# 128-row score matmuls, and the adaLN products spread over feed-forward and mixer blocks, in a two-layer macaron trunk

## The chip, the cores and the metric

The program runs on one core of one Trainium2 chip. The metric is device time in microseconds, the median of the runs shown; lower is better. Engines are named as in the profile: PE is TensorE (PEld its weight loads), DVE VectorE, ACT ScalarE, POOL GpSimd, SP SyncE, whose queue issues nearly all DMAs.

## What is computed

Two layers of three sub-layers each, on x of 512 tokens by 1024, in fp32:

```
c1 = silu(c)                                     # one vector of 1024
for l in range(2):
    mod = c1 @ ada_w[l] + ada_b[l]               # 9 vectors of 1024: (shift, scale, gate) per sub-layer
    for s in (0, 1, 2):
        h = x * (1 + scale[s]) + shift[s]
        if s == 1:  y = concat(NSA(h), gMLP(h), SSD(h)) @ w_out          # the mixer
        else:       y = (silu(h @ w1) * (h @ w3)) @ w2                    # hidden width 2816
        x = layer_norm(alpha*x + k * (1 + gate[s]) * y) * ln_g + ln_b     # k = 1 in the mixer, else 1/2
```

NSA is attention with 8 heads of 64 in 2 key groups and 3 branches: 31 compressed keys, selected blocks (here all that are causal), and a window. Each branch is softmax(q k + bias) v under a causal mask. All 18 adaLN vectors depend on c alone, so each may be made at any time before its use; together they read 75 MB of `ada_w`.

## The kernel before, in words

**Numbers.** Each fp32 matrix is split into a high and a low part, and a product is three matmuls (`mm3`, L121 to L123). Weights come as raw tiles of 128x1024 (512 KB); `wsplit` loads one (L88), optionally multiplies it by the gate row G on VectorE (L101), casts the high part on ScalarE (L103) and subtracts it on VectorE (L105). `wsplit_s` does it in two halves (L111, L116, L117). Raw tiles have four buffers in all, shared by weights and the `ada_w` tiles; the split parts have five each. Large rows (G, `lg`, `lb`, `csil`) take the eight buffers of pool `bp`.

**Sub-layers** run in the order n = 0 to 5: FFN, mixer, FFN, FFN, mixer, FFN.

**An FFN** (`ffn`) treats its 22 hidden tiles of 128 in two halves of 11. A half has an up phase, 11 tiles of 48 matmuls of 512 columns with the activation behind each (L292 to L298: tanh on ScalarE, L293, then `th`·h3 by L294, which frees the PSUM bank of h3, then the split into `ghi` and `glo`), and a down phase (`down`, L364 to L370), which multiplies by w2 with the gate row G folded in. The down phase of token block 1 accumulates into the two banks that held h3, so its first matmul waits for L294 of the last two tiles. The last four tiles of w2 are taken block by block, with `residual` or `post_norm` behind each block.

**The adaLN products.** One vector is eight products (`ada_vec`, L155): each loads 512 KB of `ada_w` and runs one VectorE instruction with c1 broadcast in `csil`, and a small instruction that reads its accumulator. A gate vector is then finished by L167, written to DRAM element by element (the DMA `mod<-mod`), and read back as a row broadcast over partitions (the DMA `G<-mod`, `gate_par`, scaled by L178). Two of the 18 vectors are made at the start, while the first tiles are fed (`feed`); the others by `bg`, a generator that the FFNs call once behind each up tile. `share` says how many vectors each sub-layer makes (seven in n=0, four in n=2, five in n=3), and `bg` makes `total` steps in 19 calls.

**A mixer** (`mixer`) projects, runs the SSD core, makes keys (`key`) and then scores, in 24 units of group p, query block and branch. A unit of the branches 1 and 2 scores four heads (L861, L862), each a pair of matmuls into one bank: K high, held in 128 rows against q high and q low, then K low in 64 rows against q high alone. There are 64 pairs in a mixer, 16 each of 512, 384, 256 and 128 columns. VectorE adds the bias and takes the maximum (L864), ScalarE exponentiates (L866), VectorE makes factors (L816 to L820) and scales (L874); TensorE transposes the result (L892) and multiplies by the values (L902). Scores are made two units ahead (LOOK). Between these, `tick` fits in other jobs: the rest of the input projections, the output projection, and a step that loads the norm rows and G (`params`).

Who stands where on each engine is settled by a scheduler that works by the program's order and its own estimates of durations; each engine then works strictly in that order, and so does each queue of DMAs.

## Time and profile before

| | before |
|---|---|
| median of 3 runs | 2165.61 us (2159.95 to 2165.88) |
| the profiled execution, its own time | 2163.19 us |
| its span, first to last instruction | 2161.5 us |
| TensorE busy | 2092.3 us, 97% |
| VectorE busy | 1344.4 us, 62% |
| ScalarE busy | 775.9 us, 36% |
| granted TensorE clock, mean | 0.989 |
| HBM read | 275.89 MB, 130 GB/s over the span |

Busy time is the sum of an engine's instructions in the span. Matmuls are pipelined, so the rate in matmuls per stretch says more of TensorE than its busy share.

### The profile page before, as it was taken

How to read it: one execution, taken by the hardware profiler on the slowest of the kernel's cores; microseconds unless marked ns; L12 is line 12 of the kernel's file. 1: busy time of each engine (PE TensorE's matmuls, PEld its weight loads, DVE VectorE, ACT ScalarE, POOL GpSimd, SP SyncE). 2: the span in 40 equal slices, each digit the busy share in tenths (PEclk: the TensorE clock that was granted, in tenths of full speed). 3: DMA queues.
4: the chain of work that ended last, by engine and by line, in shares of the span. 5: the costliest groups of instructions: out<-in, count | busy, mean ns of one | idle time of the engine just before them, and what ended most of it. 6: DMA issues, size and time to landing. Idle time of an engine off the chain costs nothing.

```text
span 2161.5 us, 26067 instructions
## 1 busy us (share of the span) xinstructions
PE 2092.3 (97%) x10024; PEld 1664.9 (77%) x10024; DVE 1344.4 (62%) x2416; ACT 775.9 (36%) x1351; POOL 29.0 (1%) x43
## 2 busy tenths in 40 slices
PE   7979997999999999999999899999999999999997
PEld 5868886887666788888888788888766668888886
DVE  6783666676767766356584736558777665444453
ACT  3321322534556622123252212225355564222222
POOL 0000000000000000000000000000000000000000
PEclk9989998999999999999999999999999999999999
DMA  9773874323211364364446527542241204223331
GB/s 334 222 236 94 230 251 130 101 88 136 79 59 40 108 218 133 97 179 153 146 138 169 171 89 225 127 127 88 88 141 59 64 1 137 90 97 98 97 97 40
DMA packets 93001, 279.74 MB, mean 129 GB/s; under 512 B 19235, under 2 KB 23587, under 8 KB 92876
## 3 DMA queue, kind: packets, MB, share of 16 engines
q1 hardware_dynamic: 92204, 275.43, 40.9%
q0 software_dynamic: 672, 2.64, 0.3%
q8 instruction: 79, 1.29, 0.2%
q14 instruction: 46, 0.38, 0.1%
HBM read 275.89 MB, written 4.76 MB: 130 GB/s over the span
## 4 chain that ended last, share of the span: by engine, by line
PE 77%; DMA 10%; DVE 8%; issue 3%; ACT 2%; POOL 0%; SPq 0%; DVEq 0%; POOLq 0%; ACTq 0%
PE h L122 10%; PE h L121 10%; PE h L123 10%; PE y L121 8%; PE y L123 8%; PE y L122 8%; DMA raw<-in_ada_w_dram 5%; DMA raw<-in_w_dram 4%; PE pj L121 3%; PE pj L122 3%; PE pj L123 3%; PE op L902 3%; PE tp L892 2%; DVE wlo L105 2%; PE S L862 2%
## 5 line engine op out<-in xcount | busy, mean ns | idle before, releaser
L103 ACT CAST whi<-raw 128x1024 fp32r<-128x1024 f32 (+1 forms) x306 | 318.1, 1046 | 682.5 <-PE h L122 196.3
L121 PE MATMUL h<-hT_hi,whi 128*128 128x512 f32 (+1 forms) x1488 | 559.1, 377 | 4.0 <-ACT hT_hi L1033 3.8
L122 PE MATMUL h<-hT_lo,whi 128*128 128x512 f32 (+1 forms) x1488 | 559.8, 376 | 0.3 <-DVE hT_lo L215 0.3
L123 PE MATMUL h<-hT_hi,wlo 128*128 128x512 f32 (+1 forms) x1488 | 559.3, 376 | 0.0
L105 DVE TENSOR_TENSOR wlo<-raw,whi 128x1024 fp32r<-128x1024 f32 (+1 forms) x306 | 370.5, 1215 | 203.4 <-ACT whi L103 203.0
L121 PEld LDWEIGHTS h<-hT_hi,whi 128*128 128x128 f32 x1488 | 280.0, 188 | 55.5 <-ACT hT_hi L1033 4.8
L122 PEld LDWEIGHTS h<-hT_lo,whi 128*128 128x128 f32 x1488 | 280.5, 188 | 51.9 <-DVE hT_lo L215 0.9
L123 PEld LDWEIGHTS h<-hT_hi,wlo 128*128 128x128 f32 x1488 | 280.4, 188 | 50.7
L155 DVE CUSTOM_DVE_ANT_0 raw<-raw,csil 128x1024 f32<-128x1024 f32 x144 | 174.8, 1221 | 156.4 <-DMA raw<-in_ada_w_dram 155.9
L121 PE MATMUL y<-whi,ghi 128*128 128x512 f32 x576 | 228.7, 397 | 32.1 <-DVE th L294 31.8
L122 PE MATMUL y<-wlo,ghi 128*128 128x512 f32 x576 | 227.1, 394 | 0.2 <-DVE wlo L105 0.2
L123 PE MATMUL y<-whi,glo 128*128 128x512 f32 x576 | 226.8, 394 | 0.0
L101 DVE TENSOR_TENSOR raw<-raw,G 128x1024 f32<-128x1024 f32 x86 | 104.7, 1222 | 88.3 <-DMA raw<-in_w_dram 88.3
L121 PEld LDWEIGHTS y<-whi,ghi 128*128 128x128 f32 x576 | 109.9, 191 | 59.2 <-DVE th L294 36.6
L297 ACT CAST ghi<-th 128x512 fp32r<-128x512 f32 x88 | 54.5, 620 | 213.2 <-DVE th L294 213.2
L122 PEld LDWEIGHTS y<-wlo,ghi 128*128 128x128 f32 x576 | 110.1, 191 | 23.4 <-DVE wlo L105 0.6
L123 PEld LDWEIGHTS y<-whi,glo 128*128 128x128 f32 x576 | 109.9, 191 | 23.3
L121 PE MATMUL pj<-hT_hi,whi 128*128 128x512 f32 x288 | 118.4, 411 | 0.0
L123 PE MATMUL pj<-hT_hi,wlo 128*128 128x512 f32 x288 | 113.4, 394 | 0.0
L122 PE MATMUL pj<-hT_lo,whi 128*128 128x512 f32 x288 | 113.2, 393 | 0.0
L294 DVE TENSOR_TENSOR th<-th,h 128x512 f32<-128x512 f32 x88 | 60.0, 682 | 41.7 <-PE h L123 40.9
L894 ACT COPY pt<-tp 128x512 f32<-128x512 f32 (+2 forms) x96 | 54.6, 581 | 85.4 <-PE tp L892 76.9
(290 smaller groups left out, 2569.3 us busy)
## 6 DMA issues: line engine op xcount, KB each, us to landing
raw<-in_w_dram SPq DMA_DIRECT2D x264, 512.0 KB, 3.6
raw<-in_ada_w_dram SPq DMA_DIRECT2D x144, 512.0 KB, 4.6
raw<-in_wS_dram SPq DMA_DIRECT2D x36, 512.0 KB, 3.8
raw<-in_cw_dram SPq DMA_DIRECT2D x16, 512.0 KB, 3.9
raw<-in_wo_dram SPq DMA_DIRECT2D x16, 512.0 KB, 3.6
T<-lane SPq DMA_DIRECT2D x16, 256.0 KB, 3.7
lg<-in_ln_g_dram SPq DMA_DIRECT2D x6, 512.0 KB, 6.0
lb<-in_ln_b_dram SPq DMA_DIRECT2D x6, 512.0 KB, 6.8
```

Source lines behind the costliest of these rows:

```text
L101: V.tensor_mul(raw, raw, gain)
L103: S.copy(hi[:, :n], raw[:, :n])
L105: V.tensor_sub(lo[:, :n], raw[:, :n], hi[:, :n].bitcast(F32))
L121: PE.matmul(o, lh, rh, start=first, stop=False)
L122: PE.matmul(o, lh, rl, start=False, stop=False)
L123: PE.matmul(o, ll, rh, start=False, stop=last)
L155: V.tensor_tensor_reduce(out=raw, in0=raw, in1=cond["c"], scale=0.5, scalar=0.0, op0=ALU.mult, op1=ALU.add, accum_out=acc[:, k:k + 1])
L294: V.tensor_mul(th, th, h3)
L297: S.copy(hi, th)
L862: PE.matmul(o, Q[g, i][r, qs], K[br][1][r, :nk], start=False, stop=True)
L894: S.copy(pt[0:n, :], tp[0:n, :])
L902: PE.matmul(op[r, :], v, pt[0:n, g * 256:(g + 1) * 256], start=(br == 0), stop=(br == 2 and kb == qb))
```

## The change

1. **Scores.** K low is made as a full tile of 128 rows in each group, the same 64 rows twice, so that both matmuls of a pair have 128 rows; the second one then adds q low times K low as well. This takes one more VectorE subtraction per half, eight in all in both mixers, and one buffer of `bp` for the second group's tiles.
2. **The adaLN products.** `share` becomes {0:4, 1:3, 2:3, 3:3, 4:3}: three vectors move into each mixer, and three FFNs make fewer. The steps of a sub-layer are dealt over 36 calls (n=0), 38 (other FFNs) or 18 (mixers); the calls come also in the down phases (seven a half, and behind each block's residual in the first), and behind each scoring unit. Each mixer makes its own `csil` ahead of its scores.
3. **Norm rows in the mixer.** `params` is split: the gate row is loaded at the place of before, the norm rows after `settle`, some steps later.

```diff
@@ ffn
                 for b in range(4):
                     down(f, w, b)
+                bg()
...
                 if half == 0:
                     residual(b, y[b], True)
+                    bg()
@@ mixer
-        Q, K = {}, {}
+        Q, K, k_lo = {}, {}, []
...
             kh = [slab("kh", dt=F32R), slab("kh", dt=F32R)]
-            kl = slab("kl", dt=F32R)
+            if not k_lo:
+                k_lo.extend(pair(bp.tile([128, 1024], F32R, tag="b", name=nm("kl"))))
+            kl = [slab("kl", dt=F32R), k_lo[br - 1]]
             for g, r, o in ((0, lo_half, hi_half), (1, hi_half, lo_half)):
                 S.copy(kh[g][r, :], ps[r, :])
-                V.tensor_sub(kl[r, :], ps[r, :], kh[g][r, :].bitcast(F32))
+                V.tensor_sub(kl[g][r, :], ps[r, :], kh[g][r, :].bitcast(F32))
+                V.tensor_sub(kl[g][o, :], ps[r, :], kh[g][r, :].bitcast(F32))
                 S.copy(kh[g][o, :], ps[r, :])
...
                 PE.matmul(o, Q[g, i][:, qs], K[br][0][g][:, :nk], start=True, stop=False)
-                PE.matmul(o, Q[g, i][r, qs], K[br][1][r, :nk], start=False, stop=True)
+                PE.matmul(o, Q[g, i][:, qs], K[br][1][g][:, :nk], start=False, stop=True)
...
             if n == GAIN_0:
-                jobs.append(step(params))
+                jobs.append(step(gate_params))
...
-        jobs += [step(settle), step(gains, range(9 - GAIN_0, 8))]
+        jobs += [step(settle), step(norm_params), step(gains, range(9 - GAIN_0, 8))]
...
+        silu_c()
         probs = [score(*u, TICK_0) for u in units[:LOOK]]
...
             else:
                 release()
+            bg()
@@ planning
-    share = {0: 7, 2: 4, 3: 5}
+    share = {0: 4, 1: 3, 2: 3, 3: 3, 4: 3}
...
+        slots = {0: 36, 1: 18, 4: 18}.get(n, 38)
...
-                if n == 0 and key == items[-3]:
+                if n == 0 and key == items[-2]:
                     yield from make_bias()
...
-            want = done[1] + 1 if more else min(total, done[0] * total // 19)
+            want = done[1] + 1 if more else min(total, done[0] * total // slots)
...
             need(l, s, 2)
-            if not last:
-                need(*subs[n + 1], 1)
-                need(*subs[n + 1], 0)
             cond.clear()
-            mixer(l, P, last, lane, params)
+            mixer(l, P, last, lane, make_bg(n, P), lambda: gate_par(l, s, P), lambda: norm_par(l, s, P))
```

How this moves instructions is shown at three places. In the rows, names end in running numbers, which differ between the kernels; a tile keeps its number from row to row of one kernel.

The first is SyncE's queue in the first half of n=0, round the first gate vector: `mod` is its write to DRAM, `G` its reading back; `raw<-in_ada_w_dram` loads for a product, `raw<-in_w_dram` a weight tile. Before, between the weights of the eighth up tile (`raw_799`, `raw_805`) and of the ninth (`raw_878`, `raw_884`) of the eleven:

```order
L88 DMA raw_746<-in_ada_w_dram 128x1024
L88 DMA raw_799<-in_w_dram 128x1024
L88 DMA raw_805<-in_w_dram 128x1024
L88 DMA mod_735<-mod_98_567 128x8x1
L88 DMA ab_741<-in_ada_b_dram 128x8
L88 DMA raw_819<-in_ada_w_dram 128x1024
L88 DMA G_737<-mod_735 128x1024
L88 DMA raw_822<-in_ada_w_dram 128x1024
L88 DMA raw_825<-in_ada_w_dram 128x1024
L88 DMA raw_878<-in_w_dram 128x1024
L88 DMA raw_884<-in_w_dram 128x1024
```

and now, where `raw_991` and `raw_997` are the weights of the eleventh and last up tile, and `raw_1086` and `raw_1126` tiles of w2:

```order
L88 DMA raw_938<-in_ada_w_dram 128x1024
L88 DMA raw_991<-in_w_dram 128x1024
L88 DMA raw_997<-in_w_dram 128x1024
L88 DMA raw_1011<-in_ada_w_dram 128x1024
L88 DMA raw_1086<-in_w_dram 128x1024
L88 DMA raw_1120<-in_ada_w_dram 128x1024
L88 DMA mod_1073<-mod_98_567 128x8x1
L88 DMA ab_1118<-in_ada_b_dram 128x8
L88 DMA G_1075<-mod_1073 128x1024
L88 DMA raw_1123<-in_ada_w_dram 128x1024
L88 DMA raw_1126<-in_w_dram 128x1024
```

The write and the reading back stood three up tiles ahead of the end of the up phase; they now stand behind its last weights, among the first tiles of w2.

The second is VectorE at the end of the up phase of the second half of n=0 (L294 is `th`·h3, L101 the product of w2 and G, L155 an adaLN product and its accumulator). Before, ahead of the last tile's L294 (`th_2387`):

```order
L101 TENSOR_TENSOR raw_2570<-raw_2570,G_737 128x1024
L298 TENSOR_TENSOR glo_2322<-th_2317,ghi_2321 128x512
L105 TENSOR_TENSOR wlo_2482<-raw_2477,whi_2480 128x1024
L105 TENSOR_TENSOR wlo_2513<-raw_2508,whi_2511 128x1024
L293 SCALAR_TENSOR_TENSOR th_2387<-th_2387,h_411_2337 128x512
L101 TENSOR_TENSOR raw_2601<-raw_2601,G_737 128x1024
L111 TENSOR_TENSOR raw_2632<-raw_2632,G_737 128x1024
L294 TENSOR_TENSOR th_2387<-th_2387,h_412_2338 128x512
L105 TENSOR_TENSOR wlo_2544<-raw_2539,whi_2542 128x1024
L298 TENSOR_TENSOR glo_2392<-th_2387,ghi_2391 128x512
```

and now, ahead of the last tile's L294 (`th_2282`):

```order
L155 ISA raw_2475,mod_374_2291<-raw_2475,csil_112 128x1024
L155 ISA mod_374_2291 128x1
L105 TENSOR_TENSOR wlo_2415<-raw_2410,whi_2413 128x1024
L293 SCALAR_TENSOR_TENSOR th_2282<-th_2282,h_368_2232 128x512
L101 TENSOR_TENSOR raw_2478<-raw_2478,G_1075 128x1024
L155 ISA raw_2509,mod_374_2291<-raw_2509,csil_112 128x1024
L155 ISA mod_374_2291 128x1
L167 SCALAR_TENSOR_TENSOR mod_374_2291<-mod_374_2291,ab_2292 128x8
L101 TENSOR_TENSOR raw_2515<-raw_2515,G_1075 128x1024
L294 TENSOR_TENSOR th_2282<-th_2282,h_369_2233 128x512
```

Before, only w2's products and splits stand round L293 and L294; now two adaLN products stand among them, and with the second L167, which ends a gate vector, two rows ahead of the last L294.

The third is VectorE in the first mixer's scores, in a unit with 128 columns. Before (L864 maximum, L816 to L820 factors, L874 scaling):

```order
L864 ISA P_4838,mx_4825<-S_4837,T_4003 128x128
L864 ISA mx_4825 128x1
L864 ISA P_4828,mx_4825<-S_4827,T_4000 128x128
L864 ISA mx_4825 128x1
L864 ISA P_4838,mx_4825<-S_4837,T_4006 128x128
L864 ISA mx_4825 128x1
L816 TENSOR_SCALAR sm_4826<-sm_4826 128x4
L817 RECIPROCAL sm_4826<-sm_4826 128x4
L820 TENSOR_TENSOR sm_4826<-sm_4826,gts_2964 128x4
L874 TENSOR_SCALAR P_4828<-P_4828,sm_4826 128x128
L874 TENSOR_SCALAR P_4838<-P_4838,sm_4826 128x128 x2
L225 SCALAR_TENSOR_TENSOR x_sb<-x_sb,y_4861 128x512
```

and now, where the same lines stand as L869, L822 to L826 and L879:

```order
L155 ISA raw_4900,mod_826_4712<-raw_4900,csil_3916 128x1024
L155 ISA mod_826_4712 128x1
L822 TENSOR_SCALAR sm_4783<-sm_4783 128x4
L155 ISA raw_4903,mod_826_4712<-raw_4903,csil_3916 128x1024
L155 ISA mod_826_4712 128x1
L823 RECIPROCAL sm_4783<-sm_4783 128x4
L155 ISA raw_4952,mod_826_4712<-raw_4952,csil_3916 128x1024
L155 ISA mod_826_4712 128x1
L826 TENSOR_TENSOR sm_4783<-sm_4783,gts_2878 128x4
L225 SCALAR_TENSOR_TENSOR x_sb<-x_sb,y_4818 128x512
L879 TENSOR_SCALAR P_4785<-P_4785,sm_4783 128x128
L879 TENSOR_SCALAR P_4795<-P_4795,sm_4783 128x128 x2
```

Three adaLN products stand between the maxima and the factors, so ahead of the scaling that TensorE's transposes take.

## Rows read from the trace of the kernel before

**Rows 1.** The page: the span, the busy time and count of each engine (section 1), and from section 2, the span in 40 slices of 54 us, the row of PE.
```profile
span 2161.5 us, 26067 instructions
...
PE 2092.3 (97%) x10024; PEld 1664.9 (77%) x10024; DVE 1344.4 (62%) x2416; ACT 775.9 (36%) x1351; POOL 29.0 (1%) x43
...
PE   7979997999999999999999899999999999999997
```

**Rows 2.** Busy time by stretch: from and to in us, its length, then for each engine busy us and in brackets how many instructions ran; the last three columns are the granted TensorE clock, the share of DMA and GB/s. First a steady stretch, then the start, then the three ends of an up phase at which TensorE ran fewer matmuls (behind each of the first two the next 40 us), and last such an end at which it did not.
```profile
200.00:240.00 40.00, 40.00 (x178) 33.14 (x177) 22.44 (x32) 8.67 (x10) 0.00 (x0) 1.00 0.62 164
0.00:40.00 40.00, 24.15 (x100) 18.95 (x101) 28.37 (x54) 16.09 (x21) 0.20 (x4) 1.00 1.00 357
120.00:160.00 40.00, 27.56 (x117) 21.88 (x116) 34.21 (x46) 11.22 (x14) 0.00 (x0) 0.87 0.66 224
160.00:200.00 40.00, 40.00 (x171) 32.90 (x171) 12.48 (x12) 7.36 (x7) 0.00 (x0) 0.96 0.30 93
320.00:360.00 40.00, 27.52 (x109) 21.73 (x108) 27.16 (x33) 8.49 (x11) 0.00 (x0) 0.80 0.53 153
360.00:400.00 40.00, 40.00 (x175) 33.04 (x174) 17.30 (x19) 10.45 (x14) 0.00 (x0) 0.98 0.41 126
1200.00:1240.00 40.00, 33.34 (x139) 27.09 (x138) 30.41 (x37) 10.92 (x14) 0.00 (x0) 0.91 0.49 158
840.00:880.00 40.00, 39.87 (x177) 32.67 (x176) 21.21 (x21) 9.43 (x11) 0.00 (x0) 1.00 0.32 95
```

**Rows 3.** TensorE's timeline at these three ends: start us, duration us, engine, line, operation and tiles; in square brackets how long the engine had stood idle before it, and what released it.
```profile
146.90 0.50 PE L121 MATMUL y<-whi,ghi 128*128 128x512 f32 x1 [1.44 <-DVE th L294]
158.69 0.80 PE L121 MATMUL y<-whi,ghi 128*128 128x512 f32 x1 [10.82 <-DVE th L294]
...
344.44 0.79 PE L121 MATMUL y<-whi,ghi 128*128 128x512 f32 x1 [3.04 <-DVE th L294]
355.52 0.80 PE L121 MATMUL y<-whi,ghi 128*128 128x512 f32 x1 [9.43 <-DVE th L294]
356.12 0.63 PE L122 MATMUL y<-wlo,ghi 128*128 128x512 f32 x1
356.54 0.63 PE L123 MATMUL y<-whi,glo 128*128 128x512 f32 x1
...
1230.93 0.79 PE L121 MATMUL y<-whi,ghi 128*128 128x512 f32 x1 [6.66 <-DVE th L294]
```

**Rows 4.** VectorE's timeline ahead of the second row of these (columns as in rows 3).
```profile
153.11 0.68 DVE L293 SCALAR_TENSOR_TENSOR th<-th,h 128x512 f32<-128x512 f32 x1
156.81 1.23 DVE L101 TENSOR_TENSOR raw<-raw,G 128x1024 f32<-128x1024 f32 x1 [1.89 <-DMA raw<-in_w_dram]
157.96 0.68 DVE L294 TENSOR_TENSOR th<-th,h 128x512 f32<-128x512 f32 x1
```

**Rows 5.** Groups of instructions by line and shape over the whole span: busy us in total, mean ns of one, then the engine's idle time just ahead of them and what ended most of it.
```profile
L155 DVE CUSTOM_DVE_ANT_0 raw<-raw,csil 128x1024 f32<-128x1024 f32 x144 | 174.8, 1221 | 156.4 <-DMA raw<-in_ada_w_dram 155.9
L583 DVE TENSOR_TENSOR kl<-pj,kh 64x512 fp32r<-64x512 f32 x8 | 5.5, 688 | 13.2 <-ACT kh L582 12.9
```

**Rows 6.** VectorE's timeline at the last products of one gate vector, and behind another one's (columns as in rows 3).
```profile
82.95 1.22 DVE L155 CUSTOM_DVE_ANT_0 raw<-raw,csil 128x1024 f32<-128x1024 f32 x1
84.09 1.22 DVE L155 CUSTOM_DVE_ANT_0 raw<-raw,csil 128x1024 f32<-128x1024 f32 x1
...
1183.85 1.23 DVE L155 CUSTOM_DVE_ANT_0 raw<-raw,csil 128x1024 f32<-128x1024 f32 x1 [12.15 <-DMA raw<-in_ada_w_dram]
```

**Rows 7.** The timeline of SyncE's DMA queue round a gate vector's write and its reading back: start us, us of issuing, engine, line, operation and tiles.
```profile
85.43 0.38 SPq L88 DMA_DIRECT2D mod<-mod  x1
...
95.80 0.33 SPq L88 DMA_DIRECT2D G<-mod  x1
```

**Rows 8.** DMA issues by tile: queue and kind, how many, KB each, median us from issue to landing.
```profile
G<-mod SPq DMA_DIRECT2D x6, 512.0 KB, 7.5
mod<-mod SPq DMA_DIRECT2D x6, 4.0 KB, 11.9
```

**Rows 9.** Busy time of each engine in the two scoring stretches, from the first score matmul to the last (columns as in rows 2), then in the stretch ahead of the first of them, in which the keys are made, and in the 40 us of the trace in which VectorE has its highest share while TensorE is never idle.
```profile
544.90:713.70 168.80, 168.74 (x847) 106.84 (x847) 119.08 (x381) 95.47 (x233) 2.77 (x3) 1.00 0.16 51
1598.90:1767.80 168.90, 168.84 (x847) 106.91 (x847) 119.19 (x382) 95.56 (x233) 2.76 (x3) 1.00 0.16 51
415.00:544.00 129.00, 126.91 (x722) 104.38 (x720) 97.91 (x205) 55.86 (x113) 2.73 (x4) 1.00 0.35 115
440.00:480.00 40.00, 40.00 (x199) 34.09 (x198) 35.81 (x77) 16.70 (x30) 1.03 (x1) 1.00 0.37 119
```

**Rows 10.** TensorE's timeline in the first scoring stretch: score matmuls of 512 columns, then of 128 (columns as in rows 3).
```profile
646.52 0.50 PE L861 MATMUL S<-kh,qa 128*128 128x512 f32 x1
646.95 0.50 PE L862 MATMUL S<-kl,qa 64*128 64x512 f32 x1
647.38 0.50 PE L861 MATMUL S<-kh,qa 128*128 128x512 f32 x1
...
640.63 0.32 PE L862 MATMUL S<-kl,qa 64*128 64x128 f32 x1
640.88 0.33 PE L861 MATMUL S<-kh,qb 128*128 128x128 f32 x1
```

**Rows 11.** What VectorE waits for in the first scoring stretch: engine, tile and line, what it waits for, us in total, times, longest us.
```profile
DVE P L864 <- PE S L862: 11.8, 20, 2.2
```

More of the change, by code (lines that the diff above doesn't have):

```diff
@@ L406, in gelu2, with mixer @@
         V.scalar_tensor_tensor(dst, t[:, :n], 1.0, src, op0=ALU.add, op1=ALU.mult)
-    def mixer(l, P, last, lane, params):
+    def mixer(l, P, last, lane, bg, gate_params, norm_params):
         p0, p1 = slab("p0"), slab("p1")
@@ L855, in score @@
             for e, (g, i) in enumerate(heads(p)):
-                r = (lo_half, hi_half)[g]
                 if e % per == 0:
```

## The prediction

> **What bounds the kernel now.** I read the page first. TensorE is busy 97% of a span of 2161.5 us [rows 1], so whatever makes the kernel shorter must make TensorE's own work shorter or fill its gaps; the row of slices shows the gaps at slices 2, 3, 7 and 23. The second view is the table of stretches, in matmuls per 40 us, since busy time flatters pipelined matmuls. A steady stretch runs 178, that is 0.225 us for a matmul of 512 columns [rows 2]. Three stretches that hold the end of an FFN's up phase run 117, 109 and 139, and the 40 us behind the first two 171 and 175, at granted clocks down to 0.80. At 0.225 us each, the missing matmuls cost 68 x 0.225 = 15.3 us, 72 x 0.225 = 16.2 us and 39 x 0.225 = 8.8 us, **40.3 us** in all. Another such end, in n=2, loses nothing (177) [rows 2]. The third view, TensorE's timeline, names the cause: waits of 1.44 and 10.82, 3.04 and 9.43, and 6.66 us, each for L294 on VectorE [rows 3], 31.4 us together. The other 8.9 us are the clock: behind the gap at 355.52 matmuls come every 0.42 us. VectorE's timeline tells why L294 is late: between the last tile's L293 at 153.11 and its L294 at 157.96 it works and waits for the products of w2 with G, one of which has to wait for its load [rows 4]. The start (100 matmuls, DMA share 1.00) [rows 2] is not touched.
>
> The fourth view is the scoring stretch of each mixer, 168.8 us. TensorE is never idle there, while VectorE is busy 119 us and DMA 16% [rows 9]. Its timeline shows what fills it: a score matmul of 512 columns follows the one ahead after 0.43 us, whether it has 128 or 64 rows, and one of 128 columns after 0.25 us [rows 10], against the 0.225 us that a 512-column matmul takes elsewhere.
>
> **Part 1, scores of 128 rows.** The pairs alternate between 128 and 64 rows, and only there does the pitch go up. If a pair of equal rows runs at the steady pitch, a pair of 512 columns takes 0.45 instead of 0.86 us (saving 0.41), and one of 128 columns, at 0.225 x 128/512 = 0.056 us each, 0.11 instead of 0.50 (saving 0.39). The saving hardly depends on width, so 64 pairs give 64 x 0.39 = **25 us of TensorE** in a mixer; its work there falls from 169 to 144 us. The bound from below is no saving at all, if the second operand and not the rows makes the pitch; the steady rows are nearest in form, so I take them. The Trainium skill, page "TensorEngine Tiling (Array Packing)", section "Performance Considerations", speaks against this part: it lists a contraction of 64 rows as the case for tiles of 64 rows. By it the 64-row form is the better one and the sum would be 2136 instead of 2116; the trace disagrees, as a 64-row matmul costs 0.43 us here and a 128-row one elsewhere 0.225.
>
> The extra subtractions are eight of 0.688 us [rows 5], 2.8 us of VectorE in each mixer. They lie in a stretch in which VectorE is busy 98 of 129 us and TensorE 127 [rows 9]; that cover makes them cost between 0 and 2.8 each, and I take 0.5, **-1 us** in all.
>
> **Part 2, in the mixers.** 24 products come to each mixer, and by the order of instructions 21 of them fall between its first and last score. One product takes VectorE 1.14 us from start to start (82.95 to 84.09) [rows 6], so VectorE's work in the stretch goes from 119 to 119 + 24 = 143 us, just as TensorE's falls to 144. Neither can be the sole bound. The floor is 144 us and the ceiling the present 169 (it could be more only if VectorE kept its present 50 us of idle time, but that is in part waiting for the scores [rows 11], which get shorter). The nearest row is the 40 us in which VectorE is busiest beside a TensorE that never idles: 35.81/40 = 0.90 [rows 9]. At that share 143 us take **159**, a gain of 10 us in each mixer, 20 in both. The loads are hidden: 24 x 0.52 MB in 159 us are 79 GB/s on top of 51 [rows 9], against 357 in the first stretch [rows 2]. `silu_c` adds one load and two instructions of 128x1024, about 1 us of VectorE, for which the same holds.
>
> **Part 2, in the FFNs.** n=0 makes 32 products instead of 56 beside its tiles, n=3 24 instead of 40, n=2 24 instead of 32. Before, three products stand in each up tile of n=0: 3.4 us of VectorE in the 48 x 0.225 = 10.8 us of the tile; now 44 steps over 36 calls leave about one. So VectorE is no longer behind when an up phase ends, and the waits of [rows 3] go. What is late next is the gate vector. Its write took from 85.43 to about 95.80, when the queue could issue the reading back [rows 7]; that lands some 5.5 us later (median 7.5) [rows 8], a chain of 16 us. At 85 us nobody waited for it. Now it is started in the eighth of the eleven tiles, at 146.90 - 1.44 - 3 x 10.8 = 113 us at the latest and a tile earlier, 102, at the soonest; I take 107. G is then there at 123, and by the order 18 VectorE instructions of 128x1024 (1.14 us) and 9 of 128x512 (0.68 us [rows 4]) still stand ahead of the last L294: 123 + 20.5 + 6.1 = 149.6, where TensorE wants it at 145.5. That leaves a wait of 4 us, with the clock behind it (40.3 lost for 31.4 of waiting) **5 us** of the 15.3, between none and 16 as the write starts at 102 or 113. At the end of the second half of n=0, which lost 16.2, two products and the next gate's write stand ahead of the last L294, but G is there: 2 us (0 to 9). In n=3's first half, 0.5. The second halves of n=2 and n=3 get a gate's write in their last tiles, as does the first mixer's end for n=2; a write there can hold the loads behind it as at 1183.85, where VectorE waited 12.15 us for a product's load [rows 6]. I take 1 us each for the two halves (0 to 9) and none for the mixer, whose weights were loaded ahead. Left: 5 + 2 + 0.5 + 1 + 1 = 9.5; gained: 40.3 - 9.5 = **31 us**, bounds 10 to 41.
>
> **Part 3, norm rows later.** Two loads of 512 KB go to a later place in a queue that is 16% loaded and before their first use: 0; without that cover one wait of 7.5 us as for G [rows 8].
>
> **The sum.** 31 + 20 - 1 = 50. The profiled execution took 2163.2 us, so 2113; the median of the runs is 2.4 us above that execution, so the forecast for a median is **2116 us**. Its own range, from the bounds of 10 to 41 in the FFNs held to their middle and of 150 to 165 us for a scoring stretch, is 2095 to 2135. About 0.3%, 6.5 us, is what a measurement can tell from no change.
>
> **The rivals.** All from the median of 2165.6.
> - Both parts at their best: all stalls go, and scores run at TensorE's floor. 40.3 + 2 x 25 - 1 = 89, so 2077. For it: two balanced engines with scores made two units ahead. Against it: the order puts three products between a unit's maxima and its factors. Chance 0.10.
> - VectorE takes over the scoring: it stays at 169 us, and only the FFNs gain, 31 - 1 = 30, so 2136. For it: 143 us of work in strict order, with waits for TensorE and ScalarE in between [rows 11]. 0.12.
> - The pitch of a score matmul stays 0.43 us with equal rows: the same 2136, by another cause. 0.03; that is the case of the page's rule named above.
> - The products are not spread in effect: the scheduler pulls the calls in the down phases ahead, and n=0 keeps its two stalls. 8.8 + 20 - 1 = 28, so 2138. For it: it did pull w2's products ahead of L294 [rows 4]. Against it: the order shows about one product per up tile. 0.09.
> - Slower: gate writes and products in the last tiles now hold up all six ends of n=0, n=2 and n=3 as at 355.52, 16.2 us each. 97 - 40 = 57 lost, 20 - 1 gained, so 2204. It turns the sign when the mean over six ends exceeds (40.3 + 19)/6 = 10 us. For it: the 12.15 us of [rows 6], and writes near four of the six ends. Against it: the end in n=2 loses nothing with products around it [rows 2], and VectorE has more slack than before. 0.08.
> - Waits in the scores drop TensorE's clock to its lower level: 144 us at 0.42 instead of 0.225 us per matmul are 269, 100 more in each mixer, 2165.6 - 30 + 200 = 2336. Against it: in the first 40 us, with 24 busy, the clock stood at 1.00 [rows 2], and it fell only behind gaps of about ten microseconds. 0.01. The Trainium skill, page "TensorE: Matmul & The Clock Gate", section "HAM oscillation — how this bites in real kernels", describes a kernel that pays this at each wait for loads; the fall at 355.52 agrees with it, and nothing here shows it in a scoring stretch.
>
> **How the numbers follow.** The forecast has 0.55, no change by unnamed causes 0.02. The range 2088 to 2150 holds the forecast and the three cases at 2136 and 2138, and leaves out the two ends at 2077 and 2204 and the last, about 0.2. Faster: 0.55 + 0.10 + 0.12 + 0.03 + 0.09 = 0.89, less 0.04 for tails of these cases, 0.85; within 0.3%, 0.06; slower, 0.08 + 0.01 = 0.09.
>
> **What would show it.** Right: second score matmuls at a pitch of 0.23 us for 512 columns; scoring stretches near 159 us, VectorE busy some 143 in them; ends of up phases at over 150 matmuls in their 40 us, with a wait of a few microseconds at most at the first. Wrong: a stretch still at 169 us with TensorE idle behind the scaling (VectorE holds it) or with a pitch of 0.43 (the rows were not the cause); waits for L294 of ten microseconds at any end; TensorE waiting at the end of a mixer for weights behind a gate's write.

## The result, and the profile after

The changed kernel takes 2113.36 us (median of 4 runs, 2109.04 to 2116.34); the kernel before, run beside it, 2165.11. The ratio is 0.9764, with a 95% interval of 0.974 to 0.9789. That is 51.8 us less, against a forecast of 2116 (50 less). The sum is right, but two of its terms are not: the scoring stretches gave 43 us instead of 20, and the feed-forward blocks about 7 instead of 31. The profiled execution is the slowest of the four, 2116.34 us.

The page first; these rows answer to [rows 1], with the clock's row of slices behind them:

```profile
span 2114.6 us, 26113 instructions
...
PE 2050.7 (97%) x10024; PEld 1658.9 (78%) x10024; DVE 1332.1 (63%) x2425; ACT 770.2 (36%) x1352; POOL 27.8 (1%) x43
...
PE   6979999999999999999999999999999999999997
...
PEclk9999999999999999999999999999999999999999
```

TensorE is still busy 97%. The busy time by stretch (from and to, length, then busy us and instruction count of each engine, the last three columns granted clock, DMA share, GB/s): the two scoring stretches and the one ahead of the first of them, which answer to [rows 9], then the ends of up phases, which answer to [rows 2]:

```profile
533.35:681.32 147.97, 146.81 (x837) 102.23 (x837) 132.40 (x423) 91.40 (x231) 2.77 (x3) 1.00 0.42 135
1571.60:1719.95 148.35, 146.90 (x838) 102.24 (x838) 132.48 (x424) 91.37 (x231) 2.77 (x3) 1.00 0.42 134
406.40:533.35 126.95, 125.32 (x718) 102.48 (x717) 100.08 (x204) 56.44 (x113) 2.58 (x4) 1.00 0.37 117
120.00:160.00 40.00, 29.00 (x124) 23.37 (x123) 31.23 (x41) 7.79 (x10) 0.00 (x0) 0.88 0.58 188
160.00:200.00 40.00, 40.00 (x169) 32.86 (x169) 20.47 (x25) 7.38 (x7) 0.00 (x0) 0.95 0.52 166
320.00:360.00 40.00, 37.65 (x159) 30.64 (x158) 27.81 (x34) 10.11 (x13) 0.00 (x0) 0.96 0.57 157
360.00:400.00 40.00, 40.00 (x183) 33.19 (x182) 22.75 (x34) 13.37 (x21) 1.11 (x2) 1.00 0.39 121
1180.00:1220.00 40.00, 38.96 (x173) 31.88 (x172) 23.80 (x27) 9.85 (x12) 0.00 (x0) 1.00 0.45 139
1000.00:1040.00 40.00, 35.17 (x144) 28.57 (x143) 19.92 (x21) 10.23 (x13) 0.00 (x0) 0.91 0.40 122
1370.00:1410.00 40.00, 35.82 (x151) 29.20 (x151) 19.07 (x20) 10.29 (x14) 0.00 (x0) 0.96 0.42 108
```

The scoring stretches have come down from 169 to 148 us with TensorE full. The first end (124 and 169 matmuls) is almost where it was (117 and 171), the second (159 and 183) and that of n=3's first half (173) are good, and two ends that hardly lost before (the second halves of n=2 and n=3, by the table below) now run 144 and 151. TensorE's timeline at these ends (as in [rows 3]; idle time ahead and what ended it in brackets):

```profile
147.47 0.50 PE L121 MATMUL y<-whi,ghi 128*128 128x512 f32 x1 [1.13 <-DVE th L294]
...
158.31 0.80 PE L121 MATMUL y<-whi,ghi 128*128 128x512 f32 x1 [9.88 <-DVE th L294]
...
344.64 0.50 PE L121 MATMUL y<-whi,ghi 128*128 128x512 f32 x1 [2.35 <-DVE th L294]
...
1008.51 0.80 PE L121 MATMUL y<-whi,ghi 128*128 128x512 f32 x1 [4.83 <-DVE th L294]
...
1382.77 0.79 PE L121 MATMUL y<-whi,ghi 128*128 128x512 f32 x1 [4.18 <-DVE th L294]
```

All are again waits for L294. What VectorE waits for ahead of the third of them, and what SyncE's queue holds there:

```profile
990.58 0.17 DVE L167 SCALAR_TENSOR_TENSOR mod<-mod,ab 128x8 f32<-128x8 f32 x1
...
998.68 1.23 DVE L101 TENSOR_TENSOR raw<-raw,G 128x1024 f32<-128x1024 f32 x1 [3.33 <-DMA raw<-in_w_dram]
...
1005.36 1.22 DVE L101 TENSOR_TENSOR raw<-raw,G 128x1024 f32<-128x1024 f32 x1 [3.72 <-DMA raw<-in_w_dram]
...
1007.77 0.68 DVE L294 TENSOR_TENSOR th<-th,h 128x512 f32<-128x512 f32 x1
```

```profile
988.84 2.07 SPq L88 DMA_DIRECT2D raw<-in_w_dram  x2
991.00 0.39 SPq L88 DMA_DIRECT2D mod<-mod  x1
991.43 0.80 SPq L88 DMA_DIRECT2D ab<-in_ada_b_dram  x1
995.41 14.53 SPq L88 DMA_DIRECT2D raw<-in_w_dram  x3
```

L167 at 990.58 ends a gate vector, its write `mod` is issued at 991.00, and then VectorE waits 3.33 and 3.72 us for two tiles of w2 and reaches L294 at 1007.77. That is the wait that the forecast took at 1 us, between 0 and 9. At the first end the write stands at 112.14 and G is read back at 122.86, 10.7 us later:

```profile
112.14 0.38 SPq L88 DMA_DIRECT2D mod<-mod  x1
...
122.86 0.33 SPq L88 DMA_DIRECT2D G<-mod  x1
```

In the scores, the second matmul of a pair now has 128 rows (L867), and the pitch (from one start to the next) is 0.23 us for 512 columns, against 0.43 in [rows 10], and 0.11 us for 128 columns, against 0.25; L155 in that stretch stands for 21 products (the last row, from the groups by line in the first scoring stretch: busy us, mean ns, idle time ahead):

```profile
608.43 0.28 PE L867 MATMUL S<-kl,qa 128*128 128x128 f32 x1
608.54 0.28 PE L866 MATMUL S<-kh,qb 128*128 128x128 f32 x1
...
628.40 0.39 PE L867 MATMUL S<-kl,qa 128*128 128x512 f32 x1
628.63 0.39 PE L866 MATMUL S<-kh,qa 128*128 128x512 f32 x1
628.87 0.40 PE L867 MATMUL S<-kl,qa 128*128 128x512 f32 x1
```

```profile
L155 DVE CUSTOM_DVE_ANT_0 raw<-raw,csil 128x1024 f32<-128x1024 f32 x21 | 25.4, 1214 | 0.0
```

By phase, the account of the 46.9 us between the two profiled spans is: the two scoring stretches 42.9, the eight down phases 7.0, what follows the scores 0.9; the two stretches between an FFN's end and the first score cost 3.5 more, and the start and the up phases, taken together, some 0.5 more.

### The profile page after: what moved, and what is told of

It is laid out like the page before. It is cut to its first block, busy times and chain, and to the rows that moved or that the text cites. A ratio compares the mean times of both kernels' runs of the same rounds, so it can differ in the third digit from the quotient of the medians.

```text
span 2114.6 us, 26113 instructions
## 1 busy us (share of the span) xinstructions
PE 2050.7 (97%) x10024; PEld 1658.9 (78%) x10024; DVE 1332.1 (63%) x2425; ACT 770.2 (36%) x1352; POOL 27.8 (1%) x43
## 4 chain that ended last, share of the span: by engine, by line
PE 77%; DMA 9%; DVE 8%; issue 3%; ACT 2%; POOL 0%; SPq 0%; POOLq 0%; DVEq 0%; ACTq 0%
PE h L121 11%; PE h L122 11%; PE h L123 11%; PE y L121 8%; PE y L123 8%; PE y L122 8%; DMA raw<-in_w_dram 5%; DMA raw<-in_ada_w_dram 3%; PE pj L121 3%; PE pj L122 3%; PE pj L123 3%; PE op L907 3%; DVE wlo L105 2%; PE tp L897 2%; PE S L866 1%
## 5 line engine op out<-in xcount | busy, mean ns | idle before, releaser
L105 DVE TENSOR_TENSOR wlo<-raw,whi 128x1024 fp32r<-128x1024 f32 (+1 forms) x306 | 371.0, 1215 | 201.1 <-ACT whi L103 200.5
L155 DVE CUSTOM_DVE_ANT_0 raw<-raw,csil 128x1024 f32<-128x1024 f32 x144 | 175.3, 1220 | 127.9 <-DMA raw<-in_ada_w_dram 127.7
L101 DVE TENSOR_TENSOR raw<-raw,G 128x1024 f32<-128x1024 f32 x86 | 105.0, 1221 | 81.8 <-DMA raw<-in_w_dram 81.7
L294 DVE TENSOR_TENSOR th<-th,h 128x512 f32<-128x512 f32 x88 | 60.2, 685 | 108.7 <-PE h L123 107.9
L871 ACT ACTIVATE P<-P,mx 128x512 f32<-128x512 f32 (+3 forms) x128 | 70.8, 556 | 9.1 <-DVE mx L869 9.1
```

The source lines that it names most:

```text
L101: V.tensor_mul(raw, raw, gain)
L105: V.tensor_sub(lo[:, :n], raw[:, :n], hi[:, :n].bitcast(F32))
L155: V.tensor_tensor_reduce(out=raw, in0=raw, in1=cond["c"], scale=0.5, scalar=0.0, op0=ALU.mult, op1=ALU.add, accum_out=acc[:, k:k + 1])
L294: V.tensor_mul(th, th, h3)
L871: S.activation(w, w, AF.Exp, bias=m, scale=-1.0, accum_out=sm[:, e:e + 1])
```

## The experiments

Theory A: TensorE alone sets the scoring stretch, so the products cost nothing there; and what holds the ends of up phases is the gate vector's write, element by element, which delays the loads near it. Theory B: VectorE shares in setting the scoring stretch; and at the ends it is held by the products that stand there and by their loads. The expectations below name their own A and B, for the question of each run.

The table gives each kernel's median (us, of four runs, but of a single one for extra8 and extra24; the ratios below are to the kernel before as it ran beside them, at 2161.9 to 2165.7), and from its trace the length of the down phases that matter (first to last down matmul, so with the wait for L294 in it; 60.4 when nothing waits) and of the two scoring stretches.

| kernel | us | n=0, 1st half | n=0, 2nd | n=2, 2nd | n=3, 1st | n=3, 2nd | scores |
|---|---|---|---|---|---|---|---|
| before | 2165.1 | 75.5 | 78.3 | 63.4 | 69.0 | 62.2 | 169.6, 169.6 |
| changed | 2113.4 | 74.4 | 66.1 | 70.2 | 61.4 | 67.9 | 148.0, 148.3 |
| scores_only | 2121.5 | 76.1 | 76.2 | 63.8 | 69.9 | 62.2 | 148.7, 148.7 |
| spread_only | 2150.6 | 72.3 | 65.4 | 70.7 | 60.9 | 67.9 | 171.0, 171.0 |
| extra8 | 2128.8 | 74.1 | 65.9 | 70.1 | 61.0 | 69.5 | 150.8, 151.1 |
| extra24 | 2174.2 | 74.1 | 65.8 | 68.1 | 61.4 | 67.9 | 173.4, 172.5 |
| gate_sooner | 2095.5 | 70.1 | 65.7 | 62.5 | 61.2 | 62.2 | 148.1, 148.3 |
| n0_up_only | 2108.4 | 67.5 | 80.4 | 62.8 | 61.8 | 62.2 | 148.2, 148.0 |
| gate_pool | 2110.3 | 71.3 | 64.4 | 70.1 | 60.7 | 67.5 | 148.4, 148.0 |
| gate_rows | 2087.3 | 61.9 | 63.2 | 62.2 | 60.7 | 62.3 | 147.3, 147.6 |
| rows_sooner | 2088.2 | 61.3 | 63.3 | 62.6 | 61.4 | 62.3 | 147.5, 148.0 |
| before_rows | 2134.1 | 61.2 | 69.7 | 63.4 | 60.0 | 62.3 | 171.1, 169.5 |
| norm_early | 2112.7 | 74.3 | 66.0 | 69.6 | 61.5 | 69.7 | 148.2, 148.6 |

### The two parts alone: scores_only, spread_only

```diff
  scores_only: before.py with the changed kernel's key() and score()
  spread_only: after.py with before's key(), and in score()
-                PE.matmul(o, Q[g, i][:, qs], K[br][1][g][:, :nk], start=False, stop=True)
+                PE.matmul(o, Q[g, i][r, qs], K[br][1][r, :nk], start=False, stop=True)
```

> The kernel before with part 1 alone (128-row scores; products placed as before). Theory A, TensorE alone sets the scoring stretch and the products cost it nothing: each stretch falls from 169 to 147 us as in the changed kernel (148), the stretches ahead of the scores get 1 to 2 us longer by the extra subtractions, the ends of the up phases stay as before; 2165 - 43 + 3 = 2125 us. Theory B, VectorE with its 21 products shares in setting the 148 us: without them the stretch falls to 144 us or below, 2118 us or less.

> The changed kernel with 64-row second score matmuls (part 1 undone), so the spread and the later norm rows alone. Theory A: scoring stretches stay at 169 us with TensorE never idle, VectorE at about 132 us or a little more; the feed-forward blocks gain about 7 us net, since one end of an up phase keeps its wait of 10 us and two new ones of 4 to 5 us appear: 2158 us. Theory B, the spread is worth the 31 us that were forecast and the widened scores cost something elsewhere: 2135 us.

Measured: 2121.5 us, ratio 0.981 [0.9796, 0.9825], and 2150.6 us, ratio 0.9942 [0.9921, 0.9962]. The scoring stretches (columns as above), of scores_only and then of spread_only:

```profile
542.40:691.10 148.70, 147.78 (x843) 103.09 (x843) 116.95 (x381) 93.34 (x233) 2.77 (x3) 1.00 0.18 57
```

```profile
527.30:698.30 171.00, 170.94 (x861) 107.26 (x860) 137.83 (x436) 96.55 (x239) 2.76 (x3) 1.00 0.39 125
```

Without a product the stretch takes 148.7 us, with 21 of them 148.0 to 148.3: they cost nothing, and TensorE sets it. So A holds for the scores. That the rows make the pitch is shown only for the alternation: no kernel here runs one 64-row matmul behind another. The spread alone is worth 11 us and the scores alone 40; together 51.8, so they add. For the spread, A's 2158 is nearer than B's 2135, and the same ends wait in it as in the changed kernel. 64-row scores bear the products nearly as well (171.0 us instead of 169.6, with VectorE at 138 of them).

### How much more VectorE takes in the scores: extra8, extra24

The edit is that of extra24; extra8 doubles only the products of the gate vector (`and j == 2` in the condition).

```diff
-            ada_dot(acc, ..., l, s * 3 + j, k)
+            for _ in range(2 if (l, s) in ((0, 2), (1, 2)) else 1):
+                ada_dot(acc, ..., l, s * 3 + j, k)
```

> The changed kernel with eight more products in each mixer: those of the gate vector are done twice. Theory A, TensorE alone sets the scoring stretch and VectorE (132 of 148 us) has room left: the stretches stay at 148 to 150 us. Theory B, VectorE already holds it at a share of 0.9: 141/0.9 = 157 us, 18 us more in all.

> The changed kernel with all 24 products of each mixer done twice. Theory A: VectorE then has 132 + 21 x 1.2 = 157 us of work, over the 148 of TensorE, so it becomes the bound at 157 to 160 us a stretch, and TensorE shows waits for VectorE: 20 to 25 us more in all. Theory B, at a share of 0.9: 175 us, 54 us more.

Measured, a single run each: 2128.8 and 2174.2 us. The first scoring stretch of extra8 and then of extra24:

```profile
531.30:682.10 150.80, 145.95 (x837) 102.58 (x837) 138.63 (x436) 90.20 (x227) 2.43 (x3) 0.99 0.50 160
```

```profile
532.90:706.40 173.50, 156.38 (x821) 106.25 (x820) 156.30 (x467) 90.56 (x224) 2.20 (x2) 0.94 0.56 185
```

With eight products more the stretch grows by 3 us, and what lies between the last score and the next up phase by 3.5 to 5; with 24 more it grows by 25, with VectorE busy 156.3 of 173.5 us. extra8 lies between the two theories, nearer A; for extra24 A's 157 to 160 is wrong and B's 175 near. It is not VectorE's work alone: TensorE idles some 17 us of this stretch, 12 of them for VectorE and the rest for ScalarE; VectorE idles 17 us too, 8.2 of them for scores; and the granted clock is 0.94 instead of 1.00, which by estimate (0.06 of 173.5 us) costs some 10 more. The products' loads are not what holds it: VectorE waits 0.7 us for them. The changed kernel has 132.4 of 148.0 us, 0.895. So TensorE sets its stretch, but eight more products, with which VectorE has 0.92, already cost something.

### When and how the gate vector is written: gate_sooner, gate_rows, gate_pool

```diff
  gate_sooner
-        slots = {0: 36, 1: 18, 4: 18}.get(n, 38)
+        slots = {0: 36, 1: 18, 4: 18}.get(n, 28)
...
+            if n == 0 and not more:
+                want = max(want, min(9, 3 * done[0]))
  gate_rows (wide is 128x32 with the vector in its first 8 columns, the rest zero)
-            load(bass.AP(tensor=d.tensor, offset=d.offset, ap=[[1, 128], [128, 8]]), acc)
+            V.transpose(rows, wide)
+            for q in range(4):
+                load(bass.AP(tensor=d.tensor, offset=d.offset + 32 * q, ap=[[128, 8], [1, 32]]),
+                     rows[32 * q:32 * q + 8, :])
  gate_pool
-            load(bass.AP(tensor=d.tensor, ...), acc)
+            G.dma_start(bass.AP(tensor=d.tensor, ...), acc)
```

> The changed kernel with the gate vectors finished sooner: in n=0 the first vector's steps go three to a call, as before, and n=2 and n=3 deal their steps over 28 calls instead of 38. Theory A, a gate vector's write near an end of an up phase holds up the loads of w2 behind it: the first end of n=0 (10 us of wait, 14 us lost) loses 0 to 5 us, the ends of the second halves of n=2 and n=3 lose none of their 7 and 6: 2113 - 10 - 12 = 2091 us. Theory B, the products that stand between the last L293 and L294 hold VectorE, not the write: the first end of n=0 keeps its 14 us, 2101 us or more.

> The changed kernel with the gate vector transposed on VectorE in blocks of 32x32 and written as 32 pieces of 128 bytes by four DMAs instead of 1024 single elements; nothing else moves. Theory A, it is the element-wise write that holds the queue: it lands in 3 us instead of 10 to 12, the two new waits in n=2 and n=3 go (12 us), the first end of n=0 gets its gate row 7 us sooner and gains 5 to 10: 2113 - 12 - 7 = 2094 us. Theory B, products and their loads near the ends are the cause: the waits stay, 2113 us.

> The changed kernel with the element-wise gate write issued from GpSimd's queue instead of SyncE's; nothing else is changed. Theory A1, the write holds up only what stands behind it in its own queue: the loads of w2 in SyncE's queue go past it, and the ends of the second halves of n=2 and n=3 fall from 70 and 68 us of down phase to 62 (12 us), the first end of n=0 keeps its wait, since G must still wait for the write: 2113 - 12 = 2101 us. Theory A2, its 1024 small packets slow the DMA engines themselves, whatever the queue: the two ends keep 68 to 70 us, 2113 us.

Measured: 2095.5 us, ratio 0.969 [0.9675, 0.9704]; 2087.3, 0.9657 [0.9642, 0.9671]; 2110.3, 0.9759 [0.9741, 0.9777]. Finishing the vectors sooner takes away the two new waits in n=2 and n=3 (70.2 and 67.9 to 62.5 and 62.2); the first end, at 70.1, lies between its two theories. Writing them in pieces of 128 bytes does the same without moving the write, and clears the first end, too, where VectorE's order changed as well (see before_rows). SyncE's queue and VectorE in gate_rows, at the place of the 995.41 above (L303 is L294 there):

```profile
974.55 1.30 SPq L88 DMA_DIRECT2D mod<-rows  x4
...
979.02 10.27 SPq L88 DMA_DIRECT2D raw<-in_w_dram  x3
```

```profile
974.31 0.21 DVE L177 STREAM_TRANSPOSE rows<-wide 128x32 f32<-128x32 f32 x1
...
975.98 1.23 DVE L101 TENSOR_TENSOR raw<-raw,G 128x1024 f32<-128x1024 f32 x1 [0.35 <-DMA raw<-in_w_dram]
...
985.98 1.23 DVE L111 TENSOR_TENSOR raw<-raw,G 128x1024 f32<-128x1024 f32 x1 [1.73 <-DMA raw<-in_w_dram]
987.12 0.68 DVE L303 TENSOR_TENSOR th<-th,h 128x512 f32<-128x512 f32 x1
```

The write is followed by weights as before, but VectorE waits 0.35 and 1.73 us for w2 instead of 3.33 and 3.72, and TensorE has no wait over 0.8 us for L294 there. At these two ends VectorE and SyncE's queue have the order of the changed kernel in both traces, but for the instructions of the new write, so the 8.0 and 5.6 us are the write's. gate_pool tells by what the write delays loads. GpSimd's queue issues it at 986.61; the tiles of w2 stay in SyncE's queue:

```profile
986.61 0.92 POOL L171 DMA_DIRECT2D mod<-mod  x1 [285.82 <-DVE mod L167]
```

```profile
995.03 1.23 DVE L101 TENSOR_TENSOR raw<-raw,G 128x1024 f32<-128x1024 f32 x1 [4.17 <-DMA raw<-in_w_dram]
...
1001.48 1.23 DVE L101 TENSOR_TENSOR raw<-raw,G 128x1024 f32<-128x1024 f32 x1 [3.48 <-DMA raw<-in_w_dram]
```

VectorE still waits 4.17 and 3.48 us, and the ends stay at 70.1 and 67.5: A2. The first of these two tiles was issued half a microsecond ahead of the write and landed 8.9 us after its issue, the second 10.5 us after (3.6 us is the median of such loads in the page of the changed kernel). So it is not the place in a queue: a load that is issued ahead of the write, and from another queue, is held as well. The Trainium skill, page "DMA: Bandwidth & Descriptors", section "Issuing engines are not separate DMA queues", has transfers run on the same 16 DMA engines and interleave, whichever engine issued them, and this trace agrees; its section "Rules for kernel authors" has a last dimension that is not contiguous lowered to one descriptor per element and advises to make it contiguous. The trace agrees: the page of gate_rows counts 13395 packets under 512 bytes, that of the changed kernel 19251. Here this is worth 26 us by the medians, 23 by the ratios to the kernel before.

### The first end of n=0: n0_up_only

```diff
  against gate_sooner
-                bg()
+                if s or l:
+                    bg()
...
-                    bg()
+                    if s or l:
+                        bg()
...
-        slots = {0: 36, 1: 18, 4: 18}.get(n, 28)
+        slots = {0: 20, 1: 18, 4: 18}.get(n, 28)
```

> The kernel with the gate vectors finished sooner, and n=0 calling its products behind up tiles alone (20 slots), so that none can be pulled between the last tile's L293 and L294. If the two products there, whose loads wait for one of the four raw tiles, hold the first end of n=0 (Theory B for this end), its down phase falls from 70 to 61 or 62 us, 2095 - 8 = 2087 us, unless the denser products bring the second end back. If G or the loads of w2 hold it (Theory A), it stays at 70 us, 2095 us.

Measured: 2108.4 us, ratio 0.9744 [0.9722, 0.9767]. Neither theory is right. In gate_sooner the first end kept a wait of 7.4 us, although G had been read back at 95; without the two products it is 4.8 (67.5 us), so they hold about a third of it, as far as two orders can be compared. What is left are waits for loads of w2's own tiles, behind which L293 and L294 stand on VectorE; SyncE's queue in turn waits 28.1 us between 118 and 153 for L105, which frees the raw tiles. No run takes this apart further. The second end got worse, 80.4 us, by a wait of 10.1 us at 397.67 that is none for L294: a gate's write now stands at 376.41, ahead of the mixer's weights, and ScalarE waits 9.27 us for one of them. By place and size it is the same cost at a third place, though no run takes it away there.

```profile
376.41 0.39 SPq L88 DMA_DIRECT2D mod<-mod  x1
...
377.52 2.39 SPq L88 DMA_DIRECT2D raw<-in_wB_dram  x2
```

```profile
389.71 1.04 ACT L103 CAST whi<-raw 128x1024 fp32r<-128x1024 f32 x1 [9.27 <-DMA raw<-in_wB_dram]
```

### Both repairs, and the pieces in the kernel before: rows_sooner, before_rows

```diff
  rows_sooner: gate_sooner and gate_rows together
  before_rows: before.py with the write of gate_rows
```

> Both repairs together: the gate vectors written in pieces of 128 bytes, and finished sooner (n=0 three steps to a call at first, n=2 and n=3 over 28 calls). Since the pieces alone left 1 to 3 us at each end, there is little to gain: 2084 to 2088 us; if finishing sooner pulls products between L293 and L294 of the first end as it did alone (wait of 7.4 us), 2093 us.

> The kernel before, with the gate vector transposed and written in pieces of 128 bytes; nothing else of the change. Theory A: before, the waits at the first two ends (12 us each) came from three products to an up tile, not from the write, so the ends of n=0 keep 75 and 78 us of down phase; in n=3, where the write preceded the end by 50 us, too: 2162 us, at most 5 less. Theory B, the write had a part in all: the three ends lose half of their 40 us, 2142 us.

Measured: 2088.2 us, ratio 0.9642 [0.9626, 0.9658], and 2134.1 us, ratio 0.9851 [0.983, 0.9873]. Sooner and in pieces is the same as in pieces alone. before_rows is the surprise: this one edit is worth 31 us in the kernel before, and its three ends fall from 75.5, 78.3 and 69.0 to 61.2, 69.7 and 60.0 us, with three products still in each up tile. There the expectation's A was wrong, and so was the forecast: it put the waits down to VectorE's load. The place where this could have been seen is VectorE's timeline of the kernel before, 12.8 us behind the write at 85.43 and 12.6 us behind that at 328.56:

```profile
98.20 1.22 DVE L155 CUSTOM_DVE_ANT_0 raw<-raw,csil 128x1024 f32<-128x1024 f32 x1 [6.86 <-DMA raw<-in_ada_w_dram]
...
99.35 0.68 DVE L294 TENSOR_TENSOR th<-th,h 128x512 f32<-128x512 f32 x1
...
334.73 0.68 DVE L293 SCALAR_TENSOR_TENSOR th<-th,h 128x512 f32<-128x512 f32 x1
341.19 1.22 DVE L101 TENSOR_TENSOR raw<-raw,G 128x1024 f32<-128x1024 f32 x1 [5.79 <-DMA raw<-in_w_dram]
...
343.71 0.68 DVE L294 TENSOR_TENSOR th<-th,h 128x512 f32<-128x512 f32 x1
```

In before_rows the first of these products and the L294 behind it (L303 there), and the product that waited 12.15 us in n=3 [rows 6], stand as follows:

```profile
91.00 1.22 DVE L155 CUSTOM_DVE_ANT_0 raw<-raw,csil 128x1024 f32<-128x1024 f32 x1
...
92.15 0.68 DVE L303 TENSOR_TENSOR th<-th,h 128x512 f32<-128x512 f32 x1
...
1155.38 1.23 DVE L155 CUSTOM_DVE_ANT_0 raw<-raw,csil 128x1024 f32<-128x1024 f32 x1 [3.09 <-DMA raw<-in_ada_w_dram]
```

How much of the 31 us is the write's alone differs by end. In n=3's first half VectorE and SyncE's queue have the order of the kernel before, but for one L293 that stands ahead of an L105: the wait of 12.15 us is 3.09, the wait of 6.66 us at the end, 47 us later, is gone, and so the 9.0 us can be put down to the write. At the second end of n=0 the order behind the write is the old one on VectorE, but for the small instructions of the new write; in SyncE's queue the write also stands behind one more tile of w2, and the 5.79 us have gone. At the first end the wait of 6.86 us is gone and L294 comes 7.2 us sooner there, 50 us ahead of the end; VectorE had little slack to make it up (34.2 us busy of 40 in [rows 2]). But from there on the scheduler also ordered VectorE differently, most in the last two tiles, in before_rows and in gate_rows, so for this end's 14.3 us the share of the write can't be told from that of the order. What the spread adds when the write is in pieces shows between before_rows and gate_rows: 6.5 us at the second end of n=0 (69.7 to 63.2), and 1.2 us or less, either way, at the others.

### Norm rows: norm_early

```diff
...
+                jobs.append(step(norm_params))
...
-        jobs += [step(settle), step(norm_params), step(gains, ...)]
+        jobs += [step(settle), step(gains, ...)]
```

> The changed kernel with part 3 undone: the norm rows are loaded right behind the gate row, as before. The forecast cost this part at nothing: 2113 us, within 3. Rival: the two loads at that place stand ahead of weights or products in SyncE's queue and delay the first scores: 2 to 8 us more.

Measured: 2112.7 us (2110.38 to 2116.82), ratio to before 0.9757 [0.9737, 0.9777], the changed kernel's being 0.9764. Part 3 is worth nothing that can be measured.

## Why the prediction was right, and where it was wrong

- **The sum.** 2116 forecast, 2113.4 measured. That it came so near is luck: two errors of the opposite sign met, +23 us in the scores and -24 in the feed-forward blocks.
- **Part 1, scores of 128 rows: right.** The pitch for 512 columns is as said, and the estimate of 25 us less TensorE work was near: 20.9 in scores_only (169.6 to 148.7), 21.5 in the changed kernel. What is missing lies at least in part in the narrow pairs: a matmul of 128 columns follows after 0.11 us, where the forecast scaled it to 0.056. A matmul of 64 rows that alternates with one of 128 costs as much as two of 128 rows or nearly so (0.43 us against twice 0.23, 0.25 against twice 0.11). The Trainium skill's page "TensorEngine Tiling (Array Packing)", section "Performance Considerations", which lists a contraction of 64 rows as a case for row tiles, is not borne out for a single one between full matmuls: 171.0 us with it, 148.0 without. Two row tiles side by side were not tried.
- **Part 2 in the mixers: the step that failed is "VectorE's work in the stretch goes from 119 to 119 + 24 = 143 us".** It went to 132.4. The 21 products are busy 25.4 us, as said, but busy time is the time in which at least one instruction runs. Added one by one, the durations in the stretch grow from 138.8 to 163.3 us, while the time in which they overlap grows from 19.7 to 30.9: on a fuller VectorE, instructions that stood apart before begin at the ends of their neighbours. The rule on it, that a stretch holds up to a share of 0.90, would have given 132.4/0.90 = 147 us, no more than TensorE needs; as a limit it is rough, since extra8 reached 0.92 for 3 us more. And TensorE's floor was put at 144, where 148.7 were measured without a product.
- **Part 2 in the FFNs: the step that failed is "So VectorE is no longer behind when an up phase ends, and the waits of [rows 3] go".** The cause of these waits was mis-named. With the gate vectors written in pieces and the products where they were, 31.9 of the 40 us go (before_rows); 9.0 of them stand where next to nothing else changed, 14.3 at the end where the order changed as well. The forecast also has "At 85 us nobody waited for it" of the first write; the row at 98.20 above has VectorE waiting 6.86 us behind it. The change moves each write and leaves it as it was, so that the waits moved with it: gone in n=3's first half and mostly at the second end of n=0, new in the second halves of n=2 and n=3. There the forecast had the right mechanism, by the row of 12.15 us, but priced it at 1 us each where 6.8 and 5.7 were lost. At the first end it said 5 us lost where 14 were: G came at 127 and not at 123, and w2's products and two adaLN products, all waiting for loads, followed.
- **The extra subtractions: -1 us forecast.** scores_only shows 0.3 and 0.7 us more ahead of the scores, as said; the changed kernel 1.4 and 2.1, spread_only -0.4 and 0.3. So the other microsecond takes both parts; TensorE waits no longer there than before, and what it is stays open.
- **The rivals.** "Both parts at their best" was half of what happened: the scores did run at TensorE's floor. "Slower by gate writes at all six ends" named what cost most: four of the six ends lost 14.0, 5.7, 9.8 and 7.5 us over the 60.4 of an undisturbed down phase, against 16.2 each.
- **The clock.** The case at 2336 did not come: the granted clock is 1.00 in both scoring stretches. Its argument, that the clock fell only behind gaps of about ten microseconds, is not what the rows show: [rows 2] has 0.91 in a stretch whose gap is 6.66 us, and extra24's scores have 0.94 with no single wait of TensorE over 2.5 us.
- **gate_rows** beats both kernels: 2087.3 us, 0.9657 of before.

## What to carry to other kernels

When an engine waits for another that is late, go on to what that one waited for just before, and from a late load to what else was in transfer at that moment: one step further would have named a 4 KB write. Before spreading work away from a wait, try the edit that takes one suspect out alone; here that gained 31 us where the spread gained 11. And when work is added to a partly idle engine, its busy time can grow by less than the sum (13 us for 25 here), since instructions that stood apart begin to overlap.

## What the runs showed of the hardware

- A write of 4 KB in 1024 pieces of 4 bytes takes 9 to 13 us (medians 11.9 and 10.5 in the two kernels). In gate_pool, where GpSimd's queue issues it, 512 KB loads from SyncE's queue that were under way with it landed after 8.9 and 10.5 us instead of 3.6; with the write in SyncE's queue, the load issued just ahead of that at 112.14 landed after 8.3 in the changed kernel. In 32 pieces of 128 bytes, by four DMAs, the row could be read back 4.8 us after the issue of the first of them (110.80 and 115.58 in gate_rows).
- Alternating matmuls of 128 and 64 rows follow each other after 0.43 us for 512 columns, whichever of the two comes, and after 0.25 us for 128; two of 128 rows after 0.23 and 0.11 ([rows 10] and above).
- VectorE could be busy 0.895 of a scoring stretch without lengthening it (132.4 of 148.0 us); with eight products more it had 0.92 of 150.8 us (extra8), with 24 more 0.90 of 173.5 (extra24), where TensorE waited on several things in turn and its granted clock was 0.94.
